# An encoder layer in fp32: the residual put into the output in DRAM by accumulating transfers, its rows scaled on ScalarE

## The chip, the cores and the metric

The kernel runs on one core of a Trainium2 chip. A core has TensorE (PE in the profile, its weight loads PEld), VectorE (DVE), ScalarE (ACT), GpSimd (POOL) and SyncE (SP), and 16 DMA engines that move what SP, ACT and POOL issue. The metric is the time of one execution in device microseconds (us), as the median of three runs.

## The reference

One encoder layer is applied to two batches with the same weights, x_prompt (1024 rows of 1024) and x_sample (512 rows of 1024):

```python
h = rms_norm(x, pre_w)
cols = jnp.einsum('bsd,dc->bsc', h, w_in)
# branch A: bidirectional mLSTM, branch B: dilated window attention, each times a SiLU gate
merged = g[:, :, 0] * p_m + g[:, :, 1] * p_a
out = jnp.einsum('bsd,de->bse', merged.astype(x.dtype), w_out)
return x + rms_norm(out, post_w)
```

The change concerns the last line alone: the normalised rows of `out`, times `post_w`, are added to the rows of `x`.

## The kernel before

The two batches are called A (x_prompt, 8 tiles of 128 rows) and B (x_sample, 4 tiles). Every matrix product in fp32 is made of three matmuls on split operands (`mm3`, lines 233 to 235). The program has these stages:

1. The start: x_prompt is read from DRAM, normalised and transposed, and the first columns of the weights (`w_vp`, L2362 and L2353) are read and split into a high part on ACT and a low part on DVE (L496, L497). SP issues the loads. Behind them on SP stand the stores of the value columns to scratch in DRAM (`vs_a`, L633); POOL issues the later value weights (`w_vw`, L525).
2. The pairs: the other columns of A in pairs of 128 (loop at L2433), then gate columns and the norm of B.
3. The mixers of A and B, in which dense work (weights of B, projections and output products) is filled in between the small products of the mLSTM and the attention, so that TensorE has an order written out by hand: `Fill` takes so many steps of eight or fewer matmuls per round.
4. The end: attention of B with the output product of A's first 512 rows beside it, `combine` of B beside the output product of A's other 512 rows, and last, alone, the projections and the output product of B.

The output product and the norm behind it are the function `final` (L2239), called for (A, 0), (A, 1) and (B, 0), 512 rows each. For each half u of the columns and each tile t of 128 rows it adds up eight k steps in a PSUM bank (name `dense`). At the last one `close` (L2258) takes the sum of squares on ACT (L2261), and the product with the post norm's weights on DVE (L2263 for u = 0 into `sw`, L2268 for u = 1 into `mg`). At u = 1 the two halves' sums are added on DVE (L2266), POOL takes the power -1/2 (L2267, one number a row, in `ss`), and DVE scales each half by it and adds x in the same instruction (L2271), in place into a buffer `xo` that holds x. Two of these run per tile, 24 in the kernel.

The buffers `xo` come from `xo_next` (L2228): pairs of 128x512 tiles, of which two are allotted for good (L2544), one from the bias tables of attention B while they are idle (L1958), and one for the last stage (L2549). POOL issues their loads ahead of need (L2298), 24 of 256 KB. The finished halves go to y as 24 stores of 256 KB, held in a list for two ticks and issued by SP (`pending`, L2272 and L249).

TensorE's order is written out by hand everywhere, SP's from stage 3 on; the rest is ordered by a scheduler. The weights of stage 3 and 4 come in units of 512 KB: two raw buffers (`wraw`, L285, issued by POOL in stage 4), split by ACT (L296) and DVE (L302) into five pairs of split buffers (`wh`, `wl`, and the tiles X and Q), up to four units ahead of their use.

Of the kernel before, what the change touches and what calls it, by code (L numbers as in the profile page):

```python
# [22 lines left out]
F32 = mybir.dt.float32  # L23
F32R = mybir.dt.float32r
AF = mybir.ActivationFunctionType
OP = mybir.AluOpType
# [3 lines left out]
P = 128  # L30
D = 1024
KT = D // P
BLK = 512
# [171 lines left out]
class Net:  # L205
# [1701 lines left out]
    def attend(self, T, fill, steps, first, banks, outs, after=None, beside=None, at=()):  # L1907
# [3 lines left out]
        nc = self.nc  # L1911
        self.lag = 3
        with ExitStack() as st:
# [34 lines left out]
            tiles = []  # L1948
            fill.stage(steps, 12 * T.n)

            self.xo_end = fill.done + steps

            def ready(u):
                nonlocal bias
                if u == 4 and T.n <= 4:
                    b = [x[F32] for x in bias.bufs]
                    bias = Rot(self, [b[i][:, c:c + 256].bitcast(F32R) for i in range(2) for c in (0, 256)])
                    self.xo_bufs.insert(0, ("stage", b[2:]))  # L1958
                at = len(self.queued)
                qkv = first if u == 0 else self.att_load(T, u)  # L1960
                mid = len(self.queued)
                made = self.attention(T, u, qkv, bias, sb, ps)
                if T.n > 4:
                    self.queued[at:] = self.queued[mid:] + self.queued[at:mid]
                return made
# [32 lines left out]
            if T.n > 4:  # L1998
                self.wraw = [x for x in self.wraw if x is not raw]
                self.deep = 1  # L2000
            if T.n <= 4:
                self.xo_bufs = [x for x in self.xo_bufs if x[0] != "stage"]

    def att_round(self, tiles, fill):

# [219 lines left out]
                             lambda: self.split(T, b, 8, [(1 - odd, 1, 2)], ya, 3), 4)  # L2225
                + [Unit([(a["w_pa"][ct],) for ct in range(KT // 2)], proj_a)])

    def xo_next(self, fill):  # L2228


        for i, (which, bufs) in enumerate(self.xo_bufs):
            if which != "stage" or fill.done + 14 < self.xo_end:
                break
        x = self.xo_bufs.pop(i)
        self.xo_bufs.append(x)
        self.flush(lambda p: p[3] == ("xo", x[0]))
        return x

    def final(self, T, b):  # L2239

        nc, a = self.nc, self.a
        m = self.rows[T, b] = []

        def make(weights):
            sb = self.osb
            fill = weights.__self__
            self.flush(lambda p: p[3] is not None and p[3][0] is self.sw)
            o = [x[F32] for x in self.sw.bufs]
            ss = sb.tile([P, 4, 8], F32, name="ss", bufs=2)
            if self.postw is None:  # L2250
                self.postw = sb.tile([P, D], F32, name="postw")
                with self.tc.issue_after(self.loaded.ins):
                    self.side.dma_start(self.postw, a["postw"][0:1].to_broadcast([P, D]))
                nc.scalar.mul(self.postw, self.postw, math.sqrt(D))
            pw = self.postw
            xo = {}

            def close(u, t, c, p):  # L2258
                r0 = b * BLK + t * P
                o1 = sb.tile([P, BLK], F32, name="mg", bufs=2) if u else o[t]  # L2260
                nc.scalar.activation(o1, p, AF.Square, accum_out=ss[:, t, u:u + 1])  # L2261
                if u == 0:
                    self.evicted = nc.vector.tensor_mul(o[t], p, pw[:, c])  # L2263
                    return
                which, xt = xo[t]
                nc.vector.scalar_tensor_tensor(ss[:, t, 5:6], ss[:, t, 0:1], 4 * EPS * D, ss[:, t, 1:2], op0=OP.add, op1=OP.add)  # L2266
                nc.gpsimd.tensor_tensor(ss[:, t, 6:7], ss[:, t, 5:6], self.mhalf[:, :1], op=OP.pow)  # L2267
                self.evicted = nc.vector.tensor_mul(o1, p, pw[:, c])  # L2268
                for hf, x in enumerate((o[t], o1)):
                    c2 = slice(hf * BLK, (hf + 1) * BLK)  # L2270
                    nc.vector.scalar_tensor_tensor(xt[hf], x, ss[:, t, 6:7], xt[hf], op0=OP.mult, op1=OP.add)  # L2271
                    self.pending.append((self.clock + 2, "y", (T.y[r0:r0 + P, c2], xt[hf]), ("xo", which)))  # L2272
                if t == 3 and (T, b) == self.last:
                    self.flush(lambda p: p[1] == "y")


            w, p = {}, {}
            for slot in range(2 * 8 + 2):
                for i in (slot // 2 - 1, slot // 2):
                    u, t = divmod(i, 4)  # L2280
                    if not 0 <= i < 8:
                        continue
                    kp = slot - 2 * i
                    if t == 0:
                        w[u, kp] = [x.rearrange("p (k c) -> p k c", c=BLK) for x in weights(u == kp == 0)]
                    if kp == 0:
                        p[i] = self.dense()
                    wk = w[u, kp]
                    c, ts = slice(u * BLK, (u + 1) * BLK), slice(t * P, (t + 1) * P)
                    for k in (2 * kp, 2 * kp + 1):  # L2290
                        hi, lo = m[k // 4]
                        self.mm3(p[i], (hi[:, k % 4, ts], lo[:, k % 4, ts]), (wk[0][:, k % 2], wk[1][:, k % 2]),
                                 k == 0, k == KT - 1)
                        if k == 1 and u == 1:
                            xo[t] = self.xo_next(fill)
                            for hf, x in enumerate(xo[t][1]):
                                with self.tc.issue_after(self.loaded.ins):
                                    self.side.dma_start(x, T.x[b * BLK + t * P:b * BLK + (t + 1) * P, hf * BLK:(hf + 1) * BLK])  # L2298
                        if k == KT - 1:
                            close(u, t, c, p.pop(i))  # L2300
                        if t == 3 and k % 2 == 1:
                            fill.release()
                        yield
        return Unit([(a["w_out"][i],) for i in range(8)], make)


# [4 lines left out]
def body(tc, a):  # L2311
# [3 lines left out]
    with ExitStack() as st:  # L2315
# [12 lines left out]
        with ExitStack() as s1:  # L2328
# [83 lines left out]
            with ExitStack() as s4:  # L2412
# [14 lines left out]
                        nc.scalar.dma_start(A.gt[br, ct + i], z)  # L2427

                with ExitStack() as s3:
                    cp = N.pool(s3, "c", 3, "right")  # L2430
                    wk = N.pool(s3, "work", 4, "right")
                    w = lambda dt=F32: wk.tile([P, 2 * BLK], F32R, name="pwk").bitcast(dt)
                    for kind, i in ([("att", j) for j in range(0, 24, 2)]  # L2433
# [4 lines left out]
                        weights = (coming or N.pair_weights(ua, ub, sb))[0]  # L2438
                        coming = None
                        c = N.unit_pair(weights, H, sb, cp, ps)  # L2440
                        v = [x[:, 1:1 + A.S] for x in c]
                        if kind == "att":
                            for j in range(2):
# [27 lines left out]
        with ExitStack() as s1:  # L2471
# [72 lines left out]
            N.xo_bufs = [(i, [N.osb.tile([P, BLK], F32, name=f"xo{i}{j}") for j in range(2)]) for i in range(2)]  # L2544
# [4 lines left out]
            N.xo_bufs.insert(0, ("late", [end.tile([P, BLK], F32, name=f"xo2{i}") for i in range(2)]))  # L2549
# [70 lines left out]
```

## Time and profile before

| | |
|---|---|
| median of 3 runs | 2188.33 us (2188.16 to 2189.93) |
| span of the profiled execution, first to last instruction | 2185.1 us |
| busy: PE, PEld | 2173.5 us (99%), 1857.3 us (85%) |
| busy: DVE, ACT, POOL | 1460.8 us (67%), 1085.1 us (50%), 704.2 us (32%) |
| moved by DMA | 395.62 MB, 181 GB/s on average |

The profile gives one execution. Its span is 3.2 us below the runs' median, since a run's time also holds what lies before the first and behind the last instruction; the profiled execution has no other time of its own on the page. A row of a timeline gives the start and the length of an instruction in us, the engine, the line, the operation, the tile written and the tile read, and in brackets how long the engine had been idle before it and what released it. SPq and ACTq are the issue of a transfer on these engines; issue of a transfer on POOL counts as POOL's own time. The row "DMA to landing" gives the time from the issue of a transfer to the arrival of its last byte.

### The profile page before, as it was taken

To read this page: it belongs to the slowest core of one execution; us is meant where nothing else is said; L and a number is where in the kernel's file an instruction comes from. 1 tells how busy PE (TensorE), PEld (TensorE's weight loads), DVE (VectorE), ACT (ScalarE), POOL (GpSimd) and SP (SyncE) were. 2 spreads that over 40 slices of the span, in tenths; PEclk is the share of its full clock that TensorE was granted. 3 is DMA by queue.
4 is the path that set the end of the run, shared out by engine and by line. 5 is a ranking of instruction groups with operands and counts; after the bars stand their busy time and mean duration, and the time that the engine had idled before them with its cause. 6 is when DMAs were issued, how large, how long until landed. Compare 5 with 4: busy or idle time off the path is not lost.

```text
span 2185.1 us, 33611 instructions
## 1 busy us (share of the span) xinstructions
PE 2173.5 (99%) x11626; PEld 1857.3 (85%) x11626; DVE 1460.8 (67%) x2927; ACT 1085.1 (50%) x2228; POOL 704.2 (32%) x989
## 2 busy tenths in 40 slices
PE   9999999999999999999999999999999999999998
PEld 8988888888888888888888889999788888888887
DVE  8766564657778555547888775574668855656674
ACT  7322333444444343446777656666756544554332
POOL 1000332333333222326776650011045522232331
PEclk9999999999999999999999999999999999999999
DMA  3642454733333222367646558877668786776772
GB/s 139 193 139 73 146 162 144 227 110 116 107 115 114 75 82 97 135 216 261 202 164 225 175 167 262 240 241 196 203 233 278 248 288 205 229 261 187 242 240 106
DMA packets 205748, 395.62 MB, mean 181 GB/s; under 512 B 36393, under 2 KB 117993, under 8 KB 205578
## 3 DMA queue, kind: packets, MB, share of 16 engines
q1 hardware_dynamic: 175272, 281.39, 40.2%
q0 software_dynamic: 26704, 99.50, 13.8%
q10 hardware_dynamic: 3602, 12.59, 1.4%
q8 instruction: 92, 1.51, 0.3%
q14 instruction: 78, 0.64, 0.1%
HBM read 274.71 MB, written 118.69 MB: 180 GB/s over the span
## 4 chain that ended last, share of the span: by engine, by line
PE 97%; DVE 1%; ACT 1%; DMA 1%; issue 0%; POOL 0%; DVEq 0%; POOLq 0%; ACTq 0%
PE d L233 14%; PE d L235 14%; PE d L234 14%; PE dense L233 13%; PE dense L234 13%; PE dense L235 13%; PE lg L1801 2%; PE pt L1831 2%; PE o L1874 1%; PE num L233 1%; PE num L235 1%; PE num L234 1%; PE num L1494 1%; PE o L1853 1%; PE a L1201 1%; PE kv L233 1%
## 5 line engine op out<-in xcount | busy, mean ns | idle before, releaser
L233 PE MATMUL dense<-H,wh 128*128 128x512 f32 x664 | 269.3, 406 | 0.0
L234 PE MATMUL dense<-H,wh 128*128 128x512 f32 x664 | 260.3, 392 | 0.0
L235 PE MATMUL dense<-H,wl 128*128 128x512 f32 x664 | 260.2, 392 | 0.0
L233 PE MATMUL d<-Hh,phla 128*128 128x512 f32 x608 | 236.5, 389 | 0.0
L235 PE MATMUL d<-Hh,phla 128*128 128x512 f32 x608 | 236.5, 389 | 0.0
L234 PE MATMUL d<-Hl,phla 128*128 128x512 f32 x608 | 236.5, 389 | 0.0
L302 DVE TENSOR_TENSOR wl<-wraw,wh 128x1024 fp32r<-128x1024 f32 (+1 forms) x121 | 150.8, 1248 | 57.9 <-ACT wh L296 57.8
L235 PE MATMUL d<-Hh,phlb 128*128 128x512 f32 x456 | 177.4, 389 | 0.0
L233 PE MATMUL d<-Hh,phlb 128*128 128x512 f32 x456 | 177.4, 389 | 0.0
L234 PE MATMUL d<-Hl,phlb 128*128 128x512 f32 x456 | 177.4, 389 | 0.0
L296 ACT ACTIVATE wh<-wraw 128x1024 fp32r<-128x1024 f32 (+1 forms) x124 | 128.1, 1036 | 62.1 <-PE dense L234 24.3
L235 PEld LDWEIGHTS dense<-H,wl 128*128 128x128 f32 x664 | 124.7, 188 | 28.1
L782 POOL TENSOR_TENSOR psum_w<-pw_raw 128x512 f32<-128x512 f32 x38 | 56.7, 1492 | 271.1 <-DMA pw_raw<-w_in 259.9
L1820 DVE CUSTOM_DVE_ANT_0 ls<-lg,bias 128x256 f32<-128x256 f32 (+2 forms) x240 | 78.7, 350 | 90.3 <-PE lg L1801 61.7
L233 PEld LDWEIGHTS dense<-H,wh 128*128 128x128 f32 x664 | 125.0, 188 | 16.4 <-issue 1.2
L234 PEld LDWEIGHTS dense<-H,wh 128*128 128x128 f32 x664 | 125.2, 189 | 14.7
L235 PEld LDWEIGHTS d<-Hh,phla 128*128 128x128 f32 x608 | 114.1, 188 | 23.7
L234 PEld LDWEIGHTS d<-Hl,phla 128*128 128x128 f32 x608 | 114.1, 188 | 23.7
L233 PEld LDWEIGHTS d<-Hh,phla 128*128 128x128 f32 x608 | 114.1, 188 | 23.7
L800 POOL TENSOR_TENSOR psum_w<-pw_raw,psum_w 128x512 f32<-128x512 f32 x38 | 49.3, 1298 | 254.2 <-DVE phla L764 254.2
L1824 ACT ACTIVATE ls<-ls,nm 128x256 f32<-128x256 f32 (+1 forms) x192 | 87.3, 456 | 70.2 <-DVE nm L1822 47.0
L233 PE MATMUL d<-v,Hh 128*128 128x484 f32 (+1 forms) x336 | 121.3, 361 | 0.1
(665 smaller groups left out, 5838.8 us busy)
## 6 DMA issues: line engine op xcount, KB each, us to landing
pw_raw<-w_in SPq DMA_DIRECT2D x76, 512.0 KB, 3.9
wraw<-w_in SPq DMA_DIRECT2D x63, 512.0 KB, 4.4
aqk_a<-pwk SPq DMA_DIRECT2D x32, 512.0 KB, 6.7
wraw<-w_pm POOLq DMA_DIRECT2D x24, 512.0 KB, 5.9
wraw<-w_out POOLq DMA_DIRECT2D x24, 512.0 KB, 3.7
Q<-aqk_a SPq DMA_DIRECT2D x20, 512.0 KB, 6.3
wraw<-w_v POOLq DMA_DIRECT2D x22, 430.0 KB, 6.5
aqk_b<-sw SPq DMA_DIRECT2D x36, 256.0 KB, 7.2
```

Of the source, the lines that this page charges most:

```text
L233: nc.tensor.matmul(out, lh, rh, start=start, stop=False, **kw)
L234: nc.tensor.matmul(out, lh, rl, start=False, stop=False, **kw)
L235: nc.tensor.matmul(out, ll, rh, start=False, stop=stop, **kw)
L296: high = nc.scalar.activation(hi[:, :n], raw[:, :n], AF.Copy)
L302: low = (self.lows or nc.vector).tensor_sub(lo[:, :n], raw[:, :n], hi[:, :n].bitcast(F32))
L782: self.nc.gpsimd.tensor_add(s[:, 0], ws[1][:, 0], ws[1][:, 1])
L800: nc.gpsimd.tensor_sub(s[:, 1], wa[:, 1], s[:, 1])
L1201: nc.tensor.matmul(p[:, c - c0], kT[:, ct, c * P:(c + 1) * P], qT[:, ct, c * P:(c + 1) * P], start=ct == 0, stop=ct == 1)
L1801: nc.tensor.matmul(lg[:, hh], q[hh][:, qs], z.rearrange("p (n j) -> p n j", j=P)[:, pair], start=z is k[hh], stop=z is not k[hh])
L1820: nc.vector.tensor_tensor_reduce(out=ls[rows, hh], in0=ts["lg"][hh][rows, of], in1=bt[rows, hh, by], scale=1.0, scalar=NEG, op0=OP.add, op ...
L1824: self.held = self.held[-3:] + [nc.scalar.activation(ls[:, hh], ls[:, hh], AF.Exp, bias=nm[:, hh:hh + 1], accum_out=ot[:, 128 + hh:129 + hh])]
L1831: nc.tensor.transpose(pp[:, hh * nk + x], ts["ls"][:, hh, x * P:(x + 1) * P], self.ident)
```

## The change

x is copied to y in DRAM by 12 transfers of 512 KB, issued by SP; in the code they stand in the loop of stage 2. `final` no longer reads x and has no buffers `xo`. The square's output for u = 1 goes into a tile of its own (`yo`, four buffers) in place of `mg`. Each half is scaled in place on ACT (an activation with the row's number as its scale) and added to y in DRAM by an accumulating transfer that POOL issues as soon as ACT is done. DVE loses 24 instructions, ACT gains 24, POOL loses 24 loads and gains 24 accumulating transfers, SP loses 24 stores and gains 12 copies.

```diff
             def close(u, t, c, p):
...
-                o1 = sb.tile([P, BLK], F32, name="mg", bufs=2) if u else o[t]
+                o1 = sb.tile([P, BLK], F32, name="yo", bufs=4) if u else o[t]
                 nc.scalar.activation(o1, p, AF.Square, accum_out=ss[:, t, u:u + 1])
...
-                which, xt = xo[t]
...
                 for hf, x in enumerate((o[t], o1)):
                     c2 = slice(hf * BLK, (hf + 1) * BLK)
-                    nc.vector.scalar_tensor_tensor(xt[hf], x, ss[:, t, 6:7], xt[hf], op0=OP.mult, op1=OP.add)
-                    self.pending.append((self.clock + 2, "y", (T.y[r0:r0 + P, c2], xt[hf]), ("xo", which)))
-                if t == 3 and (T, b) == self.last:
-                    self.flush(lambda p: p[1] == "y")
+                    nc.scalar.activation(x, x, AF.Copy, scale=ss[:, t, 6:7])
+                    nc.gpsimd.dma_start(T.y[r0:r0 + P, c2], x, accum_op=OP.add)
...
-                        if k == 1 and u == 1:
-                            xo[t] = self.xo_next(fill)
-                            for hf, x in enumerate(xo[t][1]):
-                                with self.tc.issue_after(self.loaded.ins):
-                                    self.side.dma_start(x, T.x[b * BLK + t * P:b * BLK + (t + 1) * P, hf * BLK:(hf + 1) * BLK])
...
                 with ExitStack() as s3:
+                    rows = [[z[P * t:P * (t + 1)] for z in (T.y, T.x)] for T in (A, B) for t in range(T.n)]
...
                         c = N.unit_pair(weights, H, sb, cp, ps)
+                        if rows:
+                            y, x = rows.pop(0)
+                            nc.sync.dma_start(y, x)
```

The order of TensorE's instructions is the same as before, and up to the output product of (A, 0) so are those of DVE, ACT and POOL. What moves is shown at three places.

The scheduler puts the copies on SP not at the loop in which they are written but near its front. Before, from SP's twelfth row on (`gb` is a small table of gate biases, `vs_a` the scratch of the values in DRAM):

```order
L372 DMA hnw<-hnw 128x8
L1039 DMA gb_693<-gb 128x1
L633 DMA vs_a<-vz_579 128x306
L633 DMA vs_a<-vz_580 128x306
L633 DMA vs_a<-vz_581 128x306
```

After, at the same place:

```order
L372 DMA hnw<-hnw 128x8
L1039 DMA gb_693<-gb 128x1
L2418 DMA y_prompt<-x_prompt 16x8192 x8
L2418 DMA y_sample<-x_sample 16x8192 x4
L633 DMA vs_a<-vz_579 128x306
L633 DMA vs_a<-vz_580 128x306
L633 DMA vs_a<-vz_581 128x306
```

All twelve copies stand between the loads of the start and the first store of values, which SP reaches behind them.

On POOL, in the output product of (A, 1) beside `combine` of B (`w_pm` are weights of the next projection, `og_b` what combine reads, `ss` the power -1/2), before:

```order
L285 DMA wraw_7146<-w_pm 128x1024
L2267 TENSOR_TENSOR ss<-ss,mhalf 128x1
L274 DMA V0a<-og_b 128x528 x3
L2267 TENSOR_TENSOR ss<-ss,mhalf 128x1
L2298 DMA xo_20046<-x_prompt 128x512
L2298 DMA xo_20047<-x_prompt 128x512
L285 DMA wraw_7147<-w_pm 128x1024
L2267 TENSOR_TENSOR ss<-ss,mhalf 128x1
```

After:

```order
L285 DMA wraw_7158<-w_pm 128x1024
L2249 TENSOR_TENSOR ss<-ss,mhalf 128x1
L274 DMA V0a<-og_b 128x528 x2
L2254 DMA y_prompt<-sw_7276 128x512
L274 DMA V0a<-og_b 128x528
L2254 DMA y_prompt<-yo 128x512
L2249 TENSOR_TENSOR ss<-ss,mhalf 128x1
L2254 DMA y_prompt<-sw_7277 128x512
L2254 DMA y_prompt<-yo 128x512
L285 DMA wraw_7159<-w_pm 128x1024
L2249 TENSOR_TENSOR ss<-ss,mhalf 128x1
```

Between two loads of weights stood two loads of x, which waited for a store of y to have freed their buffer; now four accumulating transfers stand there, which wait for ACT's scaling.

On POOL at the end of the program, with what each row waits for, before (the last rows before the program's end; `xo` is loaded with rows of x_sample):

```order
L2298 DMA xo_20047<-x_sample 128x512 [waits DMAHW4_49]
L2267 TENSOR_TENSOR ss<-ss,mhalf 128x1 [waits DVE_49,Pool_49]
L2298 DMA xo_17492<-x_sample 128x512 [waits DMAHW7_49,DMASW3_49,DVE_49]
L2298 DMA xo_17493<-x_sample 128x512 [waits DMAHW0_49,DMASW4_49,DVE_49]
L2267 TENSOR_TENSOR ss<-ss,mhalf 128x1 [waits DVE_49] x3
```

After:

```order
L2249 TENSOR_TENSOR ss<-ss,mhalf 128x1 [waits DVE_49]
L2254 DMA y_sample<-sw_7278 128x512 [waits DMASW1_49,Activation_49]
L2254 DMA y_sample<-yo 128x512 [waits Activation_49]
L2249 TENSOR_TENSOR ss<-ss,mhalf 128x1 [waits DVE_49]
L2254 DMA y_sample<-sw_7279 128x512 [waits DMASW3_49,Activation_49]
L2254 DMA y_sample<-yo 128x512 [waits DMASW4_49,Activation_49]
```

The last transfer of the program, which was a store issued by SP behind DVE, is now an accumulating transfer issued by POOL behind ACT.

More of the change, by code (lines that the diff above doesn't have):

```diff
@@ L1949, in attend @@
             fill.stage(steps, 12 * T.n)
-            self.xo_end = fill.done + steps
             def ready(u):
@@ L1957, in ready @@
                     bias = Rot(self, [b[i][:, c:c + 256].bitcast(F32R) for i in range(2) for c in (0, 256)])
-                    self.xo_bufs.insert(0, ("stage", b[2:]))
                 at = len(self.queued)
@@ L2000, in attend @@
                 self.deep = 1
-            if T.n <= 4:
-                self.xo_bufs = [x for x in self.xo_bufs if x[0] != "stage"]
     def att_round(self, tiles, fill):
@@ L2226, in branches @@
                 + [Unit([(a["w_pa"][ct],) for ct in range(KT // 2)], proj_a)])
[L2228 to L2237, printed above, removed]
     def final(self, T, b):
@@ L2255, in make @@
             pw = self.postw
-            xo = {}
             def close(u, t, c, p):
                 r0 = b * BLK + t * P
-                o1 = sb.tile([P, BLK], F32, name="mg", bufs=2) if u else o[t]
+                o1 = sb.tile([P, BLK], F32, name="yo", bufs=4) if u else o[t]
                 nc.scalar.activation(o1, p, AF.Square, accum_out=ss[:, t, u:u + 1])
@@ L2543, in body @@
             N.rows_in = [N.sraw[:, :BLK]] + [N.osb.tile([P, BLK], F32, name=f"ymr{i}") for i in range(2)]
-            N.xo_bufs = [(i, [N.osb.tile([P, BLK], F32, name=f"xo{i}{j}") for j in range(2)]) for i in range(2)]
             N.postw = None
@@ L2548, in body @@
             N.ps_d.append(N.pool(s1, "ps_e", 2, "left", PSUM))
-            N.xo_bufs.insert(0, ("late", [end.tile([P, BLK], F32, name=f"xo2{i}") for i in range(2)]))
             with ExitStack() as s2:
```

## The prediction

> **What bounds the kernel now.** I read the page first: the busy times and the chain that ended last.
>
> ```profile
> span 2185.1 us, 33611 instructions
> PE 2173.5 (99%) x11626; PEld 1857.3 (85%) x11626; DVE 1460.8 (67%) x2927; ACT 1085.1 (50%) x2228; POOL 704.2 (32%) x989
> PE 97%; DVE 1%; ACT 1%; DMA 1%; issue 0%; POOL 0%; DVEq 0%; POOLq 0%; ACTq 0%
> ```
>
> A busy PE need not be PE at its peak, so the second view is who PE waited for, over the whole span:
>
> ```profile
> PE d L2370 <- DMA Hh<-prew: 2.3, 1, 2.3
> PE d L476 <- ACT Hh L470: 0.5, 1, 0.5
> PE d L420 <- DVE u2b L417: 0.5, 1, 0.5
> PE d L235 <- DVE Hl L472: 0.4, 1, 0.4
> ```
>
> That is the complete list: 3.7 us, all of it in lines of the start, which the change does not touch. PE does not wait once for a weight, a bank or an eviction of the stages in which `final` stands. DVE's 24 scalings and POOL's 24 loads are thus off the path, and PE's order does not change. So the change can move the end only in three ways: what lies behind PE's last matmul gets shorter or longer; the copies disturb the start; or a new wait grows so long that PE meets it.
>
> **The tail.** The third view is the order of time behind the last matmul, all engines, with the landing of SP's last two stores:
>
> ```profile
> 2173.78 0.60 ACT L2261 ACTIVATE mg<-dense 128x512 f32<-128x512 f32 x1 [4.75 <-PE dense L235]
> 2177.43 0.39 PE L235 MATMUL dense<-Q,K 128*128 128x512 f32 x1
> 2177.86 0.60 ACT L2261 ACTIVATE mg<-dense 128x512 f32<-128x512 f32 x1 [3.39 <-PE dense L235]
> 2178.58 0.16 DVE L2266 SCALAR_TENSOR_TENSOR ss<-ss 128x1 f32<-128x1 f32 x1 [1.84 <-ACT mg L2261]
> 2178.66 0.69 DVE L2268 TENSOR_TENSOR mg<-dense,postw 128x512 f32<-128x512 f32 x1
> 2178.82 0.55 POOL L2267 TENSOR_TENSOR ss<-ss,mhalf 128x1 f32<-128x1 f32 x1 [3.53 <-DVE ss L2266]
> 2179.40 0.75 DVE L2271 SCALAR_TENSOR_TENSOR xo<-sw,ss,xo 128x512 f32<-128x512 f32 x1
> 2180.07 0.74 DVE L2271 SCALAR_TENSOR_TENSOR xo<-mg,ss,xo 128x512 f32<-128x512 f32 x1
> 2180.84 0.33 SPq L249 DMA_DIRECT2D y_sample<-xo  x1
> ...
> L249 SPq DMA_DIRECT2D y_sample<-xo x2: 332/332/332, 2180.2 to 2180.8; - x2
> DMA to landing us min/median/max: 2.0/2.0/2.0
> ```
>
> Square, sum, power, two scalings, store: the last store is issued at 2180.84 and lands 2.0 us later, at 2182.84. The span ends 2.3 us behind that, which I leave as it is.
>
> After the change everything up to the power stands (2178.82 + 0.55 = 2179.37). Then ACT scales. The row nearest to that is its copy of 128x512 out of SBUF:
>
> ```profile
> L2219 ACT ACTIVATE K<-mg x8: 616/632/633, 1881.6 to 2137.1; 128x512 fp32r<-128x512 f32 x8
> ```
>
> Two of 0.63 us in place of DVE's 0.75 and 0.74. DVE started its second 0.67 us behind its first, a little before that was over; I let ACT do likewise, at 0.55. The first runs from 2179.40 to 2180.03, the second to 2180.58; its input, DVE's product, is ready at 2178.66 + 0.69 = 2179.35. ACT is free for it: the tile before has its square at 2173.78, the same chain takes 2180.58 - 2177.86 = 2.7 us from there, 2176.5, and the last square comes at 2177.86. POOL issues the first accumulating transfer at about 2180.06 and, each issue taking 0.54 us (below), the second at 2180.6, 0.24 us earlier than SP did.
>
> How long it takes to land, no row shows: nothing in this kernel accumulates in DRAM. The rows beside it are the loads of x by POOL, 256 KB too: the pair at 2169, in quiet, and all of them (the second landing row, whose slowest fell into busy stages):
>
> ```profile
> L2298 POOL DMA_DIRECT2D xo<-x_sample x2: 537/558/580, 2169.0 to 2169.6; - x2
> DMA to landing us min/median/max: 3.1/3.2/3.3
> ...
> DMA to landing us min/median/max: 3.1/5.3/7.7
> ```
>
> Bounds: 2.0, if it lands like SP's store, and 7.7, POOL's slowest load. An accumulating transfer has to read y from DRAM, as POOL's load reads x, and to write it, as SP's store does; I take the one behind the other, 3.2 + 2.0 = 5.2 us. The last landing is then 2180.6 + 5.2 = 2185.8, **3.0 us later** than 2182.84. With the ends it is 0.2 us earlier (2180.6 + 2.0) or 5.5 us later (2180.6 + 7.7).
>
> The pair of POOL lands 1.2 us later than the pair of SP, but one reads and the other writes. The Trainium skill, "DMA: Bandwidth & Descriptors", section Specifications, has the first byte at about 1 us on GpSimd's path and about 0.6 us on SP's; by that alone the move to POOL would cost an estimated 0.4 us, and the tail would come out 0.2 us later instead of 3.0. No run here parts the first byte from the rest.
>
> **The copies at the start.** They stand on SP behind the load of `gb` and before the first store of values:
>
> ```profile
> 12.88 0.33 SPq L1039 DMA_DIRECT2D gb<-gb  x1
> 49.89 1.79 SPq L633 DMA_DIRECT2D vs_a<-vz  x4
> ...
> 13.00:18.00 5.00, 5.00 (x34) 4.86 (x34) 4.63 (x8) 4.94 (x9) 1.00 (x2) 1.00 1.03 417
> 18.00:50.00 32.00, 31.26 (x217) 29.10 (x215) 30.54 (x43) 24.79 (x50) 2.49 (x3) 1.00 0.06 20
> 50.00:60.00 10.00, 9.59 (x56) 8.76 (x56) 9.94 (x18) 3.60 (x7) 0.75 (x1) 1.00 0.66 198
> 60.00:73.00 13.00, 13.00 (x89) 13.00 (x89) 10.77 (x16) 5.82 (x9) 1.61 (x3) 1.00 0.79 231
> ```
>
> The columns of a stage are its length, the busy us of PE, PEld, DVE, ACT and POOL with their instructions, the granted clock, the share of the DMA engines and GB/s. From 13 to 18 us the loads of the start fill the engines; from 18 to 50 us they lie idle (0.06). The copies are issued from 13.2 on, behind the loads in SP's queue, and move 12 x 524,288 bytes = 6.29 MB. At the 417 GB/s of the loads that is 15 us, until 33; if reading and writing share that rate it is 30 us, until 48. Both end before 49.89. A copy from DRAM to DRAM is not in the trace, so the price is nothing by either, with the empty 32 us as the cover; if the cover is gone, see the third rival. Below nothing there is nothing to gain: no instruction of the start is removed. Above, the copies might slow the last loads, between 13 and 18 us. One of these feeds ACT here:
>
> ```profile
> 19.46 1.27 ACT L496 ACTIVATE v<-v 128x1288 fp32r<-128x1288 f32 x1
> 66.40 0.47 ACT L630 ACTIVATE vz<-co 128x322 fp32r<-128x322 f32 x1 [1.41 <-DVE co L742]
> 82.87 1.81 ACT L496 ACTIVATE v<-v 128x1936 fp32r<-128x1936 f32 x1
> ```
>
> The first has no wait before it, so its load was there; I allow up to 1 us if it comes later. The Trainium skill, on the same page ("Latency and other measured facts"), gives 207 to 214 GB/s in each direction for copies between tensors in DRAM at ordinary row pitches; by 214 the estimate is 29 us, an end at 47, and the sum stays. No row here shows it.
>
> **The middle.** ACT gains 24 x 0.63 = 15 us, spread over three output products, at a busy share of 50%, DVE loses 24 x 0.75 = 18 us. Each scaling waits for POOL's power, and in ACT's queue behind it stand the splits of weights and, in attention B, the exponentials. On POOL the transfers wait for ACT, and behind them stand loads of weights. The tightest stretch is `combine` of B:
>
> ```profile
> 2045.00:2075.00 30.00, 30.00 (x136) 24.80 (x135) 24.46 (x52) 10.17 (x19) 15.54 (x27) 1.00 0.89 294
> ...
> 2064.53 1.14 POOL L2298 DMA_DIRECT2D xo<-x_prompt  x2 [3.93 <-DMA y_prompt<-xo]
> 2065.66 0.53 POOL L285 DMA_DIRECT2D wraw<-w_pm  x1
> ...
> 2071.91 1.06 ACT L296 ACTIVATE X<-wraw 128x1024 fp32r<-128x1024 f32 x1 [3.86 <-DMA wraw<-w_pm]
> 2073.00 1.22 DVE L302 TENSOR_TENSOR X<-wraw,X 128x1024 fp32r<-128x1024 f32 x1 [1.33 <-ACT X L296]
> ...
> 2083.64 0.39 PE L233 MATMUL dense<-V0b,X 128*128 128x512 f32 x1
> ```
>
> This is one unit of weights from issue to use. Its load stood behind loads of x that waited 3.93 us for a store to free their buffer. It was split at 2074.2, and PE took it at 2083.64: 9.4 us in hand. The change removes that wait and those loads, and puts in waits for ACT, which here is busy 10.17 of 30 us. A wait like a tile's chain, 2.7 us, stays under 9.4. The DMA engines are at 0.89, and each accumulating transfer replaces a load and a store of the same bytes. I cost the middle at nothing.
>
> **The sum.** 0 at the start, 0 in the middle, +3.0 in the tail: span 2188.1. On the median, 2188.33 + 3.0 = **2191.3 us**, the 3.2 us between span and median unchanged.
>
> **The rivals.**
>
> *The accumulating transfer is slow (slower).* The addition may run in the DMA engines well below the rate of a plain move, at the very end, where nothing hides it. Issue at 2180.6 and +4.4 us on 2182.84 give the point from which it decides: a landing of 6.6 us, 1.4 over my value. At 7.7 us the time is 2193.8; at 10 us, three times POOL's quiet load, it is 2188.33 + 7.8 = 2196. For it: POOL's loads reach 7.7 us. Against: those stood among other traffic, and at the end the engines have only this pair. Chance 0.15.
>
> *The weights come late in `combine` of B (slower).* Loads on POOL's queue wait behind four accumulating transfers and their scalings, with the DMA engines at 0.89. It decides once a unit comes more than 9.4 us later than before. At 14 us PE stands 4.6 us, and with the tail the time is 2196. For it: the queue of POOL is in order, and one engine now waits for another twice per tile. Against: it drops a 3.93 us wait at the same spot. Chance 0.06.
>
> *The copies overrun the empty stretch (slower).* SP's stores at 49.89 are behind them; 6.29 MB in 49.9 - 18 = 31.9 us is 197 GB/s, and below that the stores come late. At half of it the copies end at 82. ACT writes the `vz` buffers again from 66.40 on, for which the stores must have left them; ACT would stand some 15 us in front of the weights' split, and PE behind it: 2191.3 + 15 = 2206, or 2196 if a third of that reaches PE. The later value weights, used at 82.87, would share the engines with the copies. Chance 0.05.
>
> *Faster.* The engines relieved, DVE and DMA, would have to be felt by PE. All its waits are 3.7 us, elsewhere; with a landing of 2.0 us the tail gives 0.2. Even both together, 3.9 us and a time of 2184.4, stay under 0.2%. Chance 0.04, for something the trace does not show.
>
> **How the numbers follow.** 0.2% of 2188 is 4.4 us, about what a measurement of this kernel can tell from no change. My case, landings from 2.0 to 6.6 us with start and middle hidden, gives 2188.1 to 2192.7, all within it: 0.70. The three slower rivals add up to 0.26, the faster one is 0.04. For the range I take my case from its lower end, rounded to 2188.0, and reach up to 2196, which takes in the slow transfer up to 10 us and a stall of weights of 4.6 us; left out are the faster case, most of the overrun, the ends of the other rivals and a little of my own case below, about 0.2.
>
> **What would show it.** Right: in the changed kernel's profile, PE's waits are the same few microseconds, all at the start; the share of the DMA engines between 18 and 50 us rises and falls back before 49.9; the first store of values is issued at about 50; the power of the last tile ends some 1.9 us behind the start of PE's last matmul, two scalings of 0.63 us follow on ACT, and the last transfer is issued 3.2 us behind that start and lands about 5 us later. Wrong: a landing over 6.6 us, a wait of PE for a `wh`, X or Q tile between 2045 and 2110, or copies still under way at 54 us.

## The result, and the profile after

| | before | after |
|---|---|---|
| median of 12 runs each, same chip | 2187.81 us (2186.67 to 2190.54) | 2193.07 us (2191.56 to 2194.51) |
| ratio | | 1.0023, 95% interval [1.0015, 1.0031] |

The changed kernel is slower by 5.26 us. That is a little over the 0.2% (4.4 us) that the prediction took as what a measurement of this kernel can tell from no change, and the interval reaches to both sides of that bound. The forecast was 2191.3: the result is inside the range, but the forecast was 1.8 us short and on the other side of the bound. As a change it was 2.3 us short, 3.0 against 5.26, since the kernel before ran at 2187.81 here and not at 2188.33.

The profiled execution of the changed kernel took 2193.77 us. The page:

```profile
span 2192.0 us, 33559 instructions
PE 2173.8 (99%) x11626; PEld 1857.4 (85%) x11626; DVE 1444.0 (66%) x2903; ACT 1100.5 (50%) x2252; POOL 713.0 (33%) x989
PE 92%; issue 2%; DVE 2%; DMA 2%; POOL 1%; ACT 1%; SPq 0%; POOLq 0%; DVEq 0%; ACTq 0%
```

PE's busy time is 2173.8 us, against 2173.5 before; DVE's fell by 17 us and ACT's rose by 15, as costed. The whole list of PE's waits:

```profile
PE d L2344 <- DMA Hh<-prew: 2.3, 1, 2.3
PE d L420 <- DVE u2b L417: 0.9, 1, 0.9
PE d L234 <- DVE v L497: 0.6, 1, 0.6
PE num L235 <- POOL scl L1241: 0.6, 1, 0.6
PE d L476 <- ACT Hh L470: 0.5, 1, 0.5
PE tp L2056 <- DVE Q L2051: 0.4, 1, 0.4
PE d L235 <- DVE Hl L472: 0.4, 1, 0.4
PE kv L233 <- DVE r L1294: 0.2, 1, 0.2
```

5.9 us against 3.7. The lines of the start (`d`) hold 4.7 of it; three waits of the middle, 1.2 us in all, are new. Where they come from is settled below.

The timeline behind the start of PE's last matmul:

```profile
2179.66 0.39 PE L235 MATMUL dense<-Q,K 128*128 128x512 f32 x1
2180.08 0.60 ACT L2244 ACTIVATE yo<-dense 128x512 f32<-128x512 f32 x1 [1.18 <-PE dense L235]
2180.80 0.16 DVE L2248 SCALAR_TENSOR_TENSOR ss<-ss 128x1 f32<-128x1 f32 x1 [3.32 <-ACT yo L2244]
2181.05 0.56 POOL L2249 TENSOR_TENSOR ss<-ss,mhalf 128x1 f32<-128x1 f32 x1 [0.70 <-DVE ss L2248]
2181.64 0.72 ACT L2253 ACTIVATE sw<-sw,ss 128x512 f32<-128x512 f32 x1 [0.87 <-POOL ss L2249]
2182.27 0.71 ACT L2253 ACTIVATE yo<-yo,ss 128x512 f32<-128x512 f32 x1
2182.66 0.88 POOL L2254 DMA_DIRECT2D y_sample<-sw  x1 [1.05 <-ACT sw L2253]
2183.28 1.15 POOL L2254 DMA_DIRECT2D y_sample<-yo  x1
```

And the time from issue to landing of these last two transfers; the longest is that of the very last:

```profile
DMA to landing us min/median/max: 4.8/5.1/5.5
```

From the last matmul's start to the end of the span it is 2192.0 - 2179.66 = 12.34 us; before it was 2185.1 - 2177.43 = 7.67. So the tail of this one execution is 4.7 us longer, against the 5.26 between the medians. Three pieces: the last issue comes 3.62 us behind the matmul's start (before 3.41), the transfer lands in 5.5 us (before 2.0), and the span ends 2192.0 - (2183.28 + 5.5) = 3.2 us behind that (before 2.3): +0.2, +3.5, +0.9.

The start, in the stages of before (columns as there):

```profile
13.00:18.00 5.00, 4.38 (x26) 3.80 (x27) 4.37 (x8) 3.73 (x7) 0.12 (x1) 1.00 1.03 420
18.00:50.00 32.00, 31.38 (x220) 29.60 (x219) 30.52 (x42) 24.78 (x49) 3.15 (x4) 1.00 0.64 217
```

And the twelve copies by their line: their issues, first and last start, and landing.

```profile
L2418 SPq DMA_DIRECT2D y_prompt<-x_prompt x8: 509/555/673, 14.5 to 22.6; - x8
L2418 SPq DMA_DIRECT2D y_sample<-x_sample x4: 509/548/589, 23.3 to 27.3; - x4
...
DMA to landing us min/median/max: 7.9/10.3/13.3
```

The copies fill the stretch that was empty (share 0.64 against 0.06) and are over by 27.3 + 13.3 = 40.6 us at the latest. The first store of values is issued at 51.4 us, against 49.9 before; in two versions below that have no copies it is issued at 50.9, so most of this delay isn't theirs. PE is as busy between 18 and 50 us as it was (31.38 against 31.26). Between 13 and 18 it is not (4.38 against 5.00), so the copies could still have a part in the loss.

### The profile page after: what moved, and what is told of

It reads as the page before. It is cut to its first block, busy times and chain, and to the rows that moved or that the text cites. A ratio compares the mean times of both kernels' runs of the same rounds, so it can differ in the third digit from the quotient of the medians.

```text
span 2192.0 us, 33559 instructions
## 1 busy us (share of the span) xinstructions
PE 2173.8 (99%) x11626; PEld 1857.4 (85%) x11626; DVE 1444.0 (66%) x2903; ACT 1100.5 (50%) x2252; POOL 713.0 (33%) x989
## 3 DMA queue, kind: packets, MB, share of 16 engines
q1 hardware_dynamic: 172200, 281.39, 40.6%
HBM read 274.71 MB, written 124.98 MB: 182 GB/s over the span
## 4 chain that ended last, share of the span: by engine, by line
PE 92%; issue 2%; DVE 2%; DMA 2%; POOL 1%; ACT 1%; SPq 0%; POOLq 0%; DVEq 0%; ACTq 0%
PE d L233 14%; PE d L235 14%; PE d L234 14%; PE dense L233 12%; PE dense L234 11%; PE dense L235 11%; PE lg L1801 2%; PE pt L1831 2%; PE o L1874 1%; PE num L233 1%; PE num L235 1%; PE num L234 1%; PE num L1494 1%; PE o L1853 1%; PE kv L233 1%
```

## The experiments

Two theories. The first: all of the loss lies behind the last matmul, in the accumulating transfer and in GpSimd's issuing it. The second: a part of it is made at the start or in the middle, by the copies or by the new waits. A third came up on the way: that ScalarE's place in the last chain costs more than its two rows say.

The eight experiments were run in two groups of four, each group on one chip beside 33 runs of the kernel before (2188.15 and 2188.43 us). The changed kernel has 12 runs beside 12 of the kernel before, each of the others 11. The first column is the time against the kernel before; the tail is the end of the span less the start of the last matmul, in the profiled execution.

| kernel | time, us | ratio [95%] | tail, us | tail against 7.67 |
|---|---|---|---|---|
| after | +5.26 | 1.0023 [1.0015, 1.0031] | 12.34 | +4.7 |
| before + copies | -0.34 | 0.9997 [0.9988, 1.0006] | 7.65 | 0.0 |
| after, no copies | +4.80 | 1.0020 [1.0011, 1.0029] | 12.21 | +4.5 |
| after, plain stores by GpSimd | +2.13 | 1.0008 [1.0000, 1.0017] | 9.78 | +2.1 |
| after, last block plain by SyncE | +0.61 | 1.0002 [0.9993, 1.0011] | 7.27 | -0.4 |
| after, scaling by VectorE | +3.83 | 1.0018 [1.0009, 1.0027] | 11.71 | +4.0 |
| after, last block half by SyncE | +3.17 | 1.0014 [1.0005, 1.0023] | 10.69 | +3.0 |
| before, last tile's stores by GpSimd | +1.41 | 1.0006 [0.9998, 1.0015] | 10.07 | +2.4 |
| last block as before, rest as after | +0.71 | 1.0003 [0.9995, 1.0012] | 7.92 | +0.2 |

The last column says what the first says, within about 1 us, in all nine rows, and the intervals are some 2 us wide to each side. What varies in the time is the tail.

**The copies alone.** The kernel before, with the twelve copies at their place, and its own stores of y behind them:

```diff
                         c = N.unit_pair(weights, H, sb, cp, ps)
+                        if rows:
+                            y, x = rows.pop(0)
+                            nc.sync.dma_start(y, x)
```

> The kernel before, with the twelve copies of x to y added at the place on SP where the change has them; the stores of y then overwrite them. Theory 1 (the change costs in the tail alone; the copies lie in idle time): ratio to before 1.000, at most 1 us, and the chain of the first 20 us differs from run to run by as much as in the two profiles at hand. Theory 2 (the copies slow the start, where the changed kernel's profile lies 1.46 us behind): 1.5 us or more above before, with the stretch from 13 to 20 us late by that.

Measured -0.34 us, ratio 0.9997 [0.9988, 1.0006], and a tail of 7.65. The copies cost nothing that can be measured, with 2 us to each side.

**Everything but the copies.** The changed kernel without them:

```diff
                             y, x = rows.pop(0)
-                            nc.sync.dma_start(y, x)
```

> The changed kernel without the twelve copies, so that x is not added (the transfers add to whatever y holds). Theory 1: as slow as the changed kernel, 5 us above before, with the last landing about 5.5 us behind the last issue. Theory 2: 1.5 us less than that, about 3.8 us above before.

Measured +4.80 us, ratio 1.0020 [1.0011, 1.0029]: as slow as with them. The second theory has lost the copies, from both sides.

**Plain stores in place of accumulating ones.** The changed kernel, its 24 transfers still issued by GpSimd behind ScalarE:

```diff
-                    nc.gpsimd.dma_start(T.y[r0:r0 + P, c2], x, accum_op=OP.add)
+                    nc.gpsimd.dma_start(T.y[r0:r0 + P, c2], x)
```

> The changed kernel with POOL's 24 transfers as plain stores instead of accumulating ones (x is left out of the output). Theory 1 (reading y and adding is what lands late): the last transfer lands like POOL's quiet load, 3.2 us instead of 5.1 to 5.5, issue takes 0.54 us instead of 0.9 to 1.15, and the time is about 2.5 us under the changed kernel, 2.8 us above before. Theory 3 (POOL's path is what costs, not the addition): landing stays near 5 us and the time stays 5 us above before.

Measured +2.13 us, ratio 1.0008 [1.0000, 1.0017]: a little less than the first theory's 2.8. The span is 2188.3 us. In its timeline, the last matmul and the last two issues:

```profile
2178.52 0.39 PE L235 MATMUL dense<-Q,K 128*128 128x512 f32 x1
...
2181.52 0.58 POOL L2254 DMA_DIRECT2D y_sample<-sw  x1 [1.05 <-ACT sw L2253]
2182.14 0.54 POOL L2254 DMA_DIRECT2D y_sample<-yo  x1
```

The landing of these two:

```profile
DMA to landing us min/median/max: 2.3/2.5/2.6
```

The issue stands at the same 3.62 us; the landing is 2.6 in place of 5.5. So accumulating is worth 2.9 us of landing, and 2.6 us of the tail (12.34 against 9.78). By the medians about two fifths of the loss stay without it (2.13 of 5.26), by the tails nearly half (2.1 of 4.7). The landing is also below the 3.2 that I had expected from POOL's load.

**The last block stored by SyncE.** The changed kernel, with the last block's eight transfers plain and on SyncE; the other sixteen accumulate as before:

```diff
-                    nc.gpsimd.dma_start(T.y[r0:r0 + P, c2], x, accum_op=OP.add)
+                    if (T, b) == self.last:
+                        nc.sync.dma_start(T.y[r0:r0 + P, c2], x)
+                    else:
+                        nc.gpsimd.dma_start(T.y[r0:r0 + P, c2], x, accum_op=OP.add)
```

> The changed kernel with the last eight transfers (the rows of x_sample) as plain stores issued by SP (x is left out of these rows). Theory 1: landing 2.0 us as before, the end of the span 2.3 us behind it, the time within 1 us of before. Theory 2: 1.5 to 2 us above before, all of it at the start. If the middle costs (a wait for weights or a bank), it is still there too: PE's last matmul then starts later than 2178 by more than the start explains.

Measured +0.61 us, ratio 1.0002 [0.9993, 1.0011], tail 7.27. With only the last block's transfers undone, the loss is gone: the sixteen others, the copies and all of ScalarE's scalings cost nothing that can be measured, with 2 us to each side. With plain stores by SyncE the tail is even 0.4 us shorter than before: the last issue comes 3.3 us behind the matmul's start (2181.85 - 2178.53), the store lands in 2.1, and the span of 2185.8 us ends 1.9 behind that.

**Scaling by VectorE.** The changed kernel, with the last step of the arithmetic back on VectorE:

```diff
-                    nc.scalar.activation(x, x, AF.Copy, scale=ss[:, t, 6:7])
+                    nc.vector.tensor_scalar(x, x, ss[:, t, 6:7], None, op0=OP.mult)
```

> The changed kernel with the last scaling done by VectorE again (a plain multiply in place), everything else as changed. Theory 1 (the 5 us are the transfers: landing and the end of the program behind GpSimd's last one): ScalarE's two scalings of 0.72 us stand in the place of two VectorE operations of about 0.67 us, so the last issue comes at 3.5 us behind the start of the last matmul, against 3.62, and the time stays 4.5 to 5.3 us above the kernel before, ratio 1.0020 to 1.0025. Theory 3 (ScalarE in the chain costs more than its two rows say, by the handing over from GpSimd and to GpSimd): the last issue comes at 2.6 us or earlier and the time falls to 4 us above or less, ratio 1.0018 or less.

Measured +3.83 us, ratio 1.0018 [1.0009, 1.0027]. By the time this is the third theory's figure (4 us or less), 0.7 us under the first theory's lower end, though the interval of 2.0 to 5.9 us holds both. The rows decide; the span is 2189.9 us:

```profile
2178.19 0.39 PE L235 MATMUL dense<-Q,K 128*128 128x512 f32 x1
...
2179.58 0.56 POOL L2249 TENSOR_TENSOR ss<-ss,mhalf 128x1 f32<-128x1 f32 x1 [0.94 <-DVE ss L2248]
2180.17 0.48 DVE L2253 TENSOR_SCALAR sw<-sw,ss 128x512 f32<-128x512 f32 x1
2180.57 0.48 DVE L2253 TENSOR_SCALAR yo<-yo,ss 128x512 f32<-128x512 f32 x1
2180.96 0.88 POOL L2254 DMA_DIRECT2D y_sample<-sw  x1 [0.82 <-DVE sw L2253]
2181.54 1.17 POOL L2254 DMA_DIRECT2D y_sample<-yo  x1
```

The plain multiply took 0.48 us, not the 0.67 that I had expected, and the last issue comes at 3.35 us: 0.27 earlier than behind ScalarE, far from the 2.6 of the third theory. The first transfer is issued 0.3 us behind the end of its scaling on VectorE too (2180.17 + 0.48 = 2180.65, issue at 2180.96), so that gap does not belong to ScalarE; the second follows 0.58 us behind the first and 0.49 behind its own scaling. The tail is 0.6 us shorter than the changed kernel's: 0.3 by the issue, and 0.4 by a last landing of 5.1 in place of 5.5. ScalarE's share of the loss, as far as the rows show it, is the 0.3 us of the issue; the rest of the 1.4 us between the times of this kernel and the changed one is within the two intervals.

**One accumulating transfer at the end instead of two.** In the last block the left half accumulates, the right half is a plain store of SyncE:

```diff
-                    nc.gpsimd.dma_start(T.y[r0:r0 + P, c2], x, accum_op=OP.add)
+                    if (T, b) == self.last and hf:
+                        nc.sync.dma_start(T.y[r0:r0 + P, c2], x)
+                    else:
+                        nc.gpsimd.dma_start(T.y[r0:r0 + P, c2], x, accum_op=OP.add)
```

> The changed kernel, but in the last block only the left half of each row tile goes by an accumulating transfer of GpSimd; the right half is a plain store of SyncE, and x is left out there. So one accumulating transfer of 256 KB is alone at the end, issued at 3.0 us behind the start of the last matmul instead of two at 3.0 and 3.6. Rate theory (two accumulating transfers share a rate of some 125 to 150 GB/s): alone it lands in 3.9 to 4.3 us, the span ends about 10.6 to 11.0 us behind the start of the last matmul, time 3.0 to 3.4 us above the kernel before, ratio 1.0014 to 1.0016. Latency theory (each accumulating transfer takes its 5 us whatever stands beside it): landing 4.8 to 5.5 us, span's end 11.5 to 12.1 us behind the start of the last matmul, time 3.9 to 4.4 us above, ratio 1.0018 to 1.0020.

Measured +3.17 us, ratio 1.0014 [1.0005, 1.0023], tail 10.69 (span 2191.1 us, last matmul at 2180.41): the rate theory's figures, by time and span. The landing was 4.6 us, above its 4.3 and below the other's 4.8, so it decides for neither. Against the latency theory, by which each accumulating transfer takes some 5 us whatever stands beside it, stands a pair in the changed kernel, issued at 2173.15 and 2173.76 as the tile before landed:

```profile
DMA to landing us min/median/max: 3.6/4.4/5.2
```

The first of them landed in 3.6 us, the second in 5.2. For the rate theory speaks the DMA view. First the changed kernel between 2179 and 2193 us, in 40 slices of 0.35 us (tenths of the engines' time, GB/s), and the queue's packets, MB and share of the 16 engines' time:

```profile
DMA  0019988999877495999999795500000000000000
GB/s 0 0 18 117 140 88 158 170 140 129 140 146 135 76 105 47 105 170 176 164 117 117 129 199 100 105 6 0 0 0 0 0 0 0 0 0 0 0 0 0
...
q0 software_dynamic: 576, 1.05, 55.4%
```

The same stretch of the kernel before, whose last pair of stores stands alone in it:

```profile
DMA  0000029996000000000000000000000000000000
GB/s 0 0 0 0 0 88 398 369 386 258 0 0 0 0 0 0 0 0 0 0 0 0 0 0 0 0 0 0 0 0 0 0 0 0 0 0 0 0 0 0
...
q1 hardware_dynamic: 288, 0.52, 9.9%
```

And of the kernel with one of each per tile:

```profile
DMA  0000699566964000999559841000000000000000
GB/s 0 0 0 0 240 363 240 76 94 117 164 111 82 12 0 18 351 345 146 88 88 199 158 88 18 0 0 0 0 0 0 0 0 0 0 0 0 0 0 0
...
q0 software_dynamic: 288, 0.52, 29.0%
q1 hardware_dynamic: 288, 0.52, 10.8%
```

A plain store runs at up to 398 GB/s; while accumulating transfers run, the engines are as full (9 in the digits) at mostly 90 to 200 GB/s. By the queues: 9.9% of 14 us on 16 engines for 0.52 MB is 43 us of engine time per MB, 55.4% for 1.05 MB is 118, and 29.0% for 0.52 MB is 125: 2.8 to 2.9 times as much. It is the accumulating that holds the engines, not GpSimd's queue: plain stores on that queue, in the kernel of the next experiment and in the same stretch, took as little as SyncE's.

```profile
q0 software_dynamic: 160, 0.52, 9.9%
```

In the last view of the three above SyncE's store of the last tile, at 351 and 345 GB/s, passes first, and the accumulating one follows it at about 90 to 200: this can be what its 4.6 us hold beyond the expected 4.3. In the changed kernel the last two tiles follow each other without a gap: the last transfer of the tile before was issued at 2179.20 and landed 5.7 us later, at 2184.9, when the very last had been issued for 1.6 us. That costs the very last little: behind a tile that had landed, the second of a pair took 5.2 us as well (above), against its 5.5.

**Only the last two stores by GpSimd.** The kernel before, with nothing else changed:

```diff
-                    self.pending.append((self.clock + 2, "y", (T.y[r0:r0 + P, c2], xt[hf]), ("xo", which)))
+                    if t == 3 and (T, b) == self.last:
+                        nc.gpsimd.dma_start(T.y[r0:r0 + P, c2], xt[hf])
+                    else:
+                        self.pending.append((self.clock + 2, "y", (T.y[r0:r0 + P, c2], xt[hf]), ("xo", which)))
```

> The kernel before, in which only the two stores of the very last row tile are issued by GpSimd instead of SyncE, plain, and nothing else is changed: no copies, no accumulation, no ScalarE scaling. Theory 1 (a part of the 5 us belongs to GpSimd's queue itself: a later issue, a landing of 2.3 to 2.6 us against 2.0, and an end of the program 3.6 to 4.0 us behind the last data against 2.2 to 2.6): the span's end comes 9.5 to 9.9 us behind the start of the last matmul against 7.7, time 1.8 to 2.2 us above the kernel before, ratio 1.0008 to 1.0010. Rival (the longer end belongs to the many transfers that GpSimd has issued before, or to ScalarE's scaling, not to who issues the last): end 7.7 to 8.3 us behind the last matmul, time within 0.6 us, ratio below 1.0003.

Measured +1.41 us, ratio 1.0006 [0.9998, 1.0015]. The time lies between the two expectations and would not decide alone; the profile does. Its span is 2188.9 us. From its timeline:

```profile
2178.83 0.39 PE L235 MATMUL dense<-Q,K 128*128 128x512 f32 x1
...
2181.46 0.74 DVE L2271 SCALAR_TENSOR_TENSOR xo<-mg,ss,xo 128x512 f32<-128x512 f32 x1
```

And the two stores by their line, first and last start and landing:

```profile
L2273 POOL DMA_DIRECT2D y_sample<-xo x2: 540/562/584, 2181.8 to 2182.5; - x2
...
DMA to landing us min/median/max: 2.3/2.4/2.5
```

The last store is issued 3.7 us behind the matmul's start (3.41 by SyncE), lands in 2.5 (2.0), and the span ends 2188.9 - (2182.5 + 2.5) = 3.9 us behind that (2.3): a tail of 10.07, 2.4 us more than before, for two transfers that changed hands. The tail is a little over the first theory's 9.9 and far from the rival's 8.3. The largest of the three pieces, 1.6 us, lies behind the last landing.

**The two ways joined.** The rows of x_prompt as in the changed kernel, with their eight copies; the last block as before, with loads of x, VectorE's multiply-add and SyncE's stores:

```diff
+                    if (T, b) != self.last:
+                        nc.scalar.activation(x, x, AF.Copy, scale=ss[:, t, 6:7])
+                        nc.gpsimd.dma_start(T.y[r0:r0 + P, c2], x, accum_op=OP.add)
+                        continue
                     nc.vector.scalar_tensor_tensor(xt[hf], x, ss[:, t, 6:7], xt[hf], op0=OP.mult, op1=OP.add)
```

> The two ways joined: the rows of the two blocks of the first sequence get x by the copies and accumulating transfers, with ScalarE's scaling, as in the changed kernel; the last block keeps the loads of x, VectorE's multiply-add and SyncE's stores of the kernel before. Theory 1 (all of the 5 us lie behind the last matmul): the span's end is 7.3 to 7.7 us behind the start of the last matmul, time within 1 us of the kernel before, ratio 0.9996 to 1.0004. Rival (accumulating transfers, copies or ScalarE's scalings also hold up the stages ahead of the end): time 1.5 us or more above the kernel before, ratio 1.0007 or more.

Measured +0.71 us, ratio 1.0003 [0.9995, 1.0012], tail 7.92: the first theory's time, with a tail 0.2 us above its range. It isn't faster than the kernel before either. No version here beats the kernel before by more than its interval: what the change relieves, nothing waits for.

## Why the prediction came out 1.8 us short

**What bounds it: right.** PE's order and busy time stand, and the change moves the end through the tail alone.

**The tail, by its three terms.** This is where the sum failed.

| term | predicted | measured | off by |
|---|---|---|---|
| last issue against before | -0.24 | +0.21 | 0.45 |
| landing against 2.0 | +3.2 | +3.5 | 0.3 |
| span's end behind the landing against 2.3 | 0 | +0.9 | 0.9 |
| sum | +3.0 | +4.7 | 1.7 |

The last 0.6 us between the tail's 4.7 and the medians' 5.26 lie within the interval.

*The rest behind the landing* is the step that failed most: "The span ends 2.3 us behind that, which I leave as it is." It held in the kernels here that SyncE ended. In the kernels whose last transfer is GpSimd's it is 3.1 to 3.9 us, worked out as above; in those whose last is SyncE's, 1.9 to 2.5. What the program does there in that time no view shows, so the cause below the queue stays open; that it goes with who issues the last transfer, the kernel before with its last two stores on GpSimd shows, and that accumulating transfers issued earlier by GpSimd don't do it, the two kernels show that have them and end with SyncE's stores (1.9 and 2.5).

*The last issue.* ScalarE's scaling out of SBUF took 0.72 us, not the 0.63 of its copies of the same shape, and GpSimd issues 0.30 us behind the end of what it waits for (2181.64 + 0.72 = 2182.36, issue at 2182.66), where I had let it follow at once, as SyncE does.

*The landing.* That 5.5 came so near to 5.2 is luck: I added POOL's load to SP's store, the times of two other transfers. The runs show other parts: GpSimd's queue lands a plain store of the same size in 2.5 or 2.6 us where SyncE's takes 2.0, and accumulating adds 2.9, while its packets hold the DMA engines 2.8 times as long per byte. Whether it is the reading of y that holds them, which I had in the sum, or the addition, no run parts; the profile's page counts 274.71 MB read from DRAM with accumulating and with plain transfers alike, so it does not list that reading. A rate "well below the rate of a plain move" is the mechanism of my first rival; at 5.5 us it stayed under the 6.6 from which I let it decide.

So the total passed 0.2% by three errors on the same side: 0.9 us behind the landing, 0.45 in the issue and 0.3 in the landing. A landing of 6.6 was a bound for one term with the others held; the sum of all three was what had to be compared with 4.4. The case to which I gave 0.70 ended at 2192.7 and was missed by 0.4 us; the range held because I had taken it up to 2196 for a much slower transfer and for late weights, neither of which came.

The Trainium skill, "DMA: Bandwidth & Descriptors", section "Latency and other measured facts", gives about 0.6 us to the first byte on the hardware queues and about 1 us on GpSimd's. The 0.3 to 0.5 us between the landings of the last plain stores (2.3 and 2.5 by GpSimd in the kernel before with these two moved, 2.0 by SyncE) agree with its difference of 0.4. The estimate that I made from it, a tail 0.2 us later, left out both the accumulation and the end.

**The copies: right.** Nothing at the start, shown from both sides. They took less than the 29 or 30 us of the estimates: 6.29 MB from 14.5 to at most 40.6 us is 241 GB/s or more. The Trainium skill, in the same section, has 207 to 214 GB/s in each direction for copies between tensors in DRAM, measured on tiles of 128 rows at wide row pitches; the contiguous copies here were faster than that, and for them the measurement decides. The third rival is out: its point was 197 GB/s.

**The loss between 13 and 18 us is not the change's.** PE waits there for DVE at L497, where GpSimd does a part of the subtractions beside VectorE. In the kernel before with only its last stores moved, whose start is the kernel before's, the same two instructions read:

```profile
11.12 1.55 POOL L497 TENSOR_TENSOR v<-v,v 128x644 fp32r<-128x644 f32 x1 [0.18 <-ACT v L496]
11.18 2.18 DVE L497 TENSOR_TENSOR v<-v,v 128x644 fp32r<-128x644 f32 x1
```

In the profiled execution of before it had been the other way round:

```profile
11.08 0.82 DVE L497 TENSOR_TENSOR v<-v,v 128x644 fp32r<-128x644 f32 x1
11.14 2.18 POOL L497 TENSOR_TENSOR v<-v,v 128x644 fp32r<-128x644 f32 x1 [0.30 <-ACT v L496]
```

So this varies without an edit near it, and the profile of before, 2185.1 + 1.8 = 2186.9 us, was of an execution near the lower end of its runs (the lowest of the 33 in each group took 2186.8 and 2186.9). That is also what was odd in the "3.2 us between span and median": a run's time lies 1.8 us above its span wherever both are known (here 2193.77 and 2192.0); the other 1.4 us was the distance of that execution from the median. It entered the sum on both sides and did no harm.

**The middle: right as far as can be told.** No wait for weights shows, and the second rival is out. I had said that all of PE's waits would stand at the start, and three small ones stand in the middle. Those for `scl` and `r` belong to instructions between 974 and 1292 us, long before the first accumulating transfer at 1931. The third falls where I had said that a wait would speak against me: `tp <- Q`, 0.4 us, at 2099. Q there is a product of `combine`, not weights. And the kernel before with its last two stores on GpSimd, in which nothing of the middle is changed, has it too, and one more:

```profile
PE d L234 <- DVE v L497: 0.4, 1, 0.4
PE tp L2061 <- DVE Q L2056: 0.4, 1, 0.4
PE num L1494 <- ACT X L1504: 0.3, 1, 0.3
```

With the copies alone there is none in the middle, without the copies `tp` waits 1.2 us, in the joined version 1.5. They come and go with the execution; whether the change makes them a little more frequent can't be told from one profile each. The kernel whose last block is stored by SyncE bounds their worth: it has all the rest of the change and is at +0.61 us, with an interval that holds zero.

## What to carry to other kernels

What relieves engines that nothing waits for gains nothing, and what it puts behind the last matmul is paid in full, here 4.7 of 5.3 us. When the last transfer of a program changes its queue or its kind, cost all three pieces of the tail: the hand-over to the issue, the landing, and the end of the program behind it, and compare their sum, not one of them, with the bound. An accumulating transfer can stand where other work covers it (sixteen of them cost nothing here that could be measured); at the very end it is paid for.

## What the runs showed of the hardware

- In the last block of the kernels, an accumulating transfer of 256 KB into DRAM landed in 3.6 to 4.8 us as the first of two, in 4.8 to 5.9 as the second and in 4.6 to 4.8 beside a plain store; the last two plain stores landed in 2.3 to 2.6 by GpSimd and in 2.0 to 2.1 by SyncE. In the busier stages ahead, accumulating transfers took up to 9.5. Their packets held the DMA engines 118 to 125 us per MB, those of plain stores 43 on either queue and 47 beside an accumulating transfer. Accumulating transfers took GpSimd 0.88 and 1.15 us to issue, against 0.58 and 0.54 for the plain stores.
- At the end of the kernels GpSimd began to issue a transfer 0.3 us behind the end of the instruction that it waited for, whether ScalarE's or VectorE's (0.49 once, 0.58 behind its issue before); SyncE 0.02 to 0.03.
- A program whose last transfer GpSimd had issued ended 3.1 to 3.9 us behind its landing, one that SyncE ended 1.9 to 2.5.
- Scaling 128x512 in SBUF by a number per row took 0.72 us on ScalarE and 0.48 on VectorE as a plain multiply; VectorE's multiply-add with a second tensor 0.75.
- VectorE and GpSimd, started within 0.06 us of each other on two subtractions of the same shape, took 0.82 and 2.18 us in one execution and 2.18 and 1.55 in another. The Trainium skill, "SBUF — State Buffer", section "Who interferes with whom", says that a VectorE instruction with two inputs in SBUF contends with a GpSimd instruction that reads SBUF; these rows agree, and add that which of the two is held up can change from one execution to the next.
